# Where the split weights of a narrow matrix product start in memory: 480 bytes or 64 bytes into their tiles

## The chip, the core and the metric

The kernel runs on one core of one Trainium2 chip. The metric is the device time of one execution in microseconds. Every figure of a profile below is from one profiled execution on that core.

## What is computed

A small decoder trunk of two layers on 512 tokens of width 1024, in float32. The part that matters here is the feed forward that ends each layer:

```python
def swiglu(h, w_gate_up, w_down):
    gu = h @ w_gate_up                                   # 1024 -> 2 * 2816
    return (jax.nn.silu(gu[..., :D_FF]) * gu[..., D_FF:]) @ w_down

x = x + swiglu(rms_norm(x, ln_ffn[layer]), w_gate_up[layer], w_down[layer])
```

Ahead of it stand, in layer 0, a gated delta rule mixer, in layer 1 a sliding-window attention, in both an attention to 256 memory tokens and an output projection.

## The kernel before

Activations lie transposed, 128 features on the partitions by 512 tokens, eight tiles for the width of 1024. A product with a weight matrix runs on TensorE in a reduced float32 format, so both operands are split in two: a high part `hi` (a copy into that format, by ScalarE, line 140) and a low part `lo` (the source minus the high part, by VectorE, line 153). One step of a product is then three matmuls (`mm3`, line 146): high weights by high input, high weights by low input, low weights by high input. Each is preceded by a weight load of its own, 128 columns of 4 bytes, that is 512 bytes in each partition.

Most products are **wide**: the moving input has 512 tokens. In the gate and up products of the feed forwards all but the first few columns go by **quarters** (`quarters`): two blocks of 128 columns are taken together, their weights and the inputs are cut into 2 by 2 quarters, and seven products of sums of quarters take the place of eight. The matmuls of these products are **narrow**: 256 tokens, four steps of three matmuls for a product. The inputs of the quarters are the high and low parts `h`, `l` of the normed activations, or sums of their quarters in tiles called `T`. The results go into the accumulators `g`.

The split weights of a quarter product are 512 columns wide. They come from `ring`: six places, cut from three pairs of tiles `whi`, `wlo` of 1152 elements. Each tile is the two halves of 1024 elements and 128 elements more, so that a place of 640 elements has room for 512 at any start up to 128:

```python
places.extend(tuple(x[:, i * T:(i + 1) * T + P] for x in two) for i in range(2))
...
return [x[:, shift[0]:shift[0] + T] for x in places[-1]]
```

`shift[0]` is set in `begin`, which starts one pair of column blocks. In each layer `begin` runs 19 times: nine times in the first half of the feed forward (four for gates, five for ups), ten in the second. The wide products use tiles of the same names from their first element on.

**Addresses.** What follows from the program's allocation, counted in bytes modulo 512 within a partition: all tiles `whi`, `wlo` of the shared pool start at 320, and so do `h`, `l` and `T` in both feed forwards. A quarter's input begins at a whole multiple of 1024 bytes in its tile, a step's weights at a whole multiple of 512 bytes after the place's start. So in all narrow matmuls of the feed forwards the weights lie 480 bytes beyond the input modulo 512, which is 32 bytes before it. In the wide products of the feed forwards the distance is 0. Distances in the rest of the program, between the moving operand and the weights that are loaded beside it, for narrow matmuls of the same format: in the first 40 us the products of the memory tokens have 128 (where `mh`, `ml` at 192 move past weights at 320), 384 (where weights at 320 in `whi`, `wlo` move past `mh`, `ml` as the loaded side) and 96 (the same with a pair `whi`, `wlo` of the early pool at 96). In the last 30 us the down products of the last two output blocks run in two halves of 256 tokens, at distance 0.

The order of the matmuls on TensorE is that of the program. The splits for the next products run ahead on ScalarE and VectorE, through the ring. The raw weights come by DMA from the SP queue (and two accumulating DMAs for each pair from GpSimd's queue).

Of the kernel before, what the change touches and what calls it, by code (L numbers as in the profile page):

```python
# [18 lines left out]
P = 128  # L19
# [67 lines left out]
class Builder:  # L87
# [1011 lines left out]
    def ffn(self, fp, xp, layer, h, apool, rope=False):  # L1099
# [4 lines left out]
        acts, sums, open_pairs, places, waiting, shift, sized = [], [], [], [], [], [0], []  # L1104
# [34 lines left out]
        def begin(f, up, by, tag, bufs, then):  # L1139

            o = [self.t(fp, [P, T], F32, tag, bufs) for _ in range(2)]
            steps = self.quarters(fp, [col(f + i, up) for i in range(2)], sums, by, o, ring)
            shift[0] = P - 8
            next(steps)
            while waiting:
                x = waiting.pop()
                self.nosync(self.fn(x, x, AF.Silu), self.held)
            end()
            next(steps)
            open_pairs.append((steps, then, o))  # L1150
            return o

        def end():
            if open_pairs:
                steps, then, o = open_pairs.pop()
                next(steps, None)
                for x in o:
                    then(x)
# [8 lines left out]
        for f0 in (0, half):  # L1167
# [7 lines left out]
            for f in range(f0 + 1, f0 + half, 2):  # L1175
                if f == 1:
                    g = []
                    for i in range(2):
                        for _ in range(2 - i):
                            sums.append(self.token_sums(fp, layer, len(sums), h))  # L1180
                        g.append(gate(f + i))
                    sums.append(self.token_sums(fp, layer, len(sums), h))
                else:
                    g = begin(f, 0, (self.rstd, self.rstd), "fg", 4, lambda x: self.fn(x, x, AF.Silu))
                begin(f, 1, g, "fu", 3, put)
# [432 lines left out]
```

## Time and profile before

| what | value |
|---|---|
| time, median of 3 runs | 1130.85 us (1130.81 to 1131.25) |
| span of the profiled execution, first to last instruction | 1129.4 us |
| TensorE busy | 1119.9 us, 99% of the span |
| VectorE busy | 827.6 us, 73% |
| ScalarE busy | 634.4 us, 56% |
| GpSimd busy | 73.2 us, 6% |
| granted TensorE clock, mean | 0.998 |

The profiled execution has no other time than its span; the span lies 1.45 us below the median of the runs, and that is what there is around the first and the last instruction. Busy time of matmuls counts their pipelined, modelled ends, so that the duration of one matmul (279 ns for a narrow one) is more than the distance to the next. The pace of matmuls is therefore read from the distance of starts, or from a stretch of the chain that holds nothing but matmuls, divided by their number.

### The profile page before, as it was taken

To read this page: it belongs to the slowest core of one execution; us is meant where nothing else is said; L and a number is where in the kernel's file an instruction comes from. 1 tells how busy PE (TensorE), PEld (TensorE's weight loads), DVE (VectorE), ACT (ScalarE), POOL (GpSimd) and SP (SyncE) were. 2 spreads that over 40 slices of the span, in tenths; PEclk is the share of its full clock that TensorE was granted. 3 is DMA by queue.
4 is the path that set the end of the run, shared out by engine and by line. 5 is a ranking of instruction groups with operands and counts; after the bars stand their busy time and mean duration, and the time that the engine had idled before them with its cause. 6 is when DMAs were issued, how large, how long until landed. Compare 5 with 4: busy or idle time off the path is not lost.

```text
span 1129.4 us, 19330 instructions
## 1 busy us (share of the span) xinstructions
PE 1119.9 (99%) x7339; PEld 986.1 (87%) x7339; DVE 827.6 (73%) x1553; ACT 634.4 (56%) x1285; POOL 73.2 (6%) x91
## 2 busy tenths in 40 slices
PE   9999999999999999999999999999999999999997
PEld 8888778887899988899988887788999988999986
DVE  7676976577888975588955877839999634889643
ACT  8588664456566632366643555856666422666434
POOL 0000000000021001011000000000111000111001
PEclk9999999999999999999999999999999999999999
DMA  8344252234567536377533321116687533776232
GB/s 314 109 153 149 95 131 86 85 113 145 174 167 195 143 111 169 102 191 195 134 89 102 132 75 38 53 43 180 158 201 185 144 103 105 173 190 156 77 103 87
DMA packets 72401, 151.15 MB, mean 134 GB/s; under 512 B 16956, under 2 KB 18516, under 8 KB 72308
## 3 DMA queue, kind: packets, MB, share of 16 engines
q1 hardware_dynamic: 60884, 129.21, 36.3%
q0 software_dynamic: 11136, 20.45, 11.2%
q8 instruction: 57, 0.93, 0.3%
q14 instruction: 36, 0.29, 0.1%
q10 hardware_dynamic: 288, 0.26, 0.1%
HBM read 142.94 MB, written 6.96 MB: 133 GB/s over the span
## 4 chain that ended last, share of the span: by engine, by line
PE 96%; DVE 2%; ACT 1%; DMA 0%; issue 0%; DVEq 0%; SPq 0%; ACTq 0%
PE pj L146 46%; PE g L146 38%; PE sc L146 6%; PE qk L146 3%; PE pt L146 2%; PE pt L150 1%; PE g L150 1%; DVE big L153 1%; DVE qv L156 0%; DVE btmp L153 0%; DMA early<-in_early 0%; DVE wlo L153 0%; ACT sm L134 0%; DVE T L153 0%; DVE gcr L153 0%
## 5 line engine op out<-in xcount | busy, mean ns | idle before, releaser
L140 ACT ACTIVATE whi<-wraw 128x512 fp32r<-128x512 f32 (+3 forms) x318 | 235.3, 748 | 240.6 <-PE pj L146 164.0
L153 DVE TENSOR_TENSOR wlo<-wraw,whi 128x512 fp32r<-128x512 f32 (+3 forms) x318 | 262.8, 837 | 92.7 <-ACT whi L140 85.2
L146 PE MATMUL pj<-h,whi 128*128 128x512 f32 (+1 forms) x652 | 256.4, 395 | 0.0
L146 PE MATMUL pj<-l,whi 128*128 128x512 f32 (+1 forms) x652 | 254.4, 390 | 0.0
L146 PE MATMUL pj<-h,wlo 128*128 128x512 f32 (+1 forms) x652 | 254.0, 390 | 0.0
L146 PE MATMUL g<-T,whi 128*128 128x256 f32 x1216 | 216.8, 279 | 0.0
L146 PEld LDWEIGHTS g<-T,whi 128*128 128x128 f32 x1216 | 185.1, 188 | 1.3 <-DVE fu L156 1.3
L146 PE MATMUL g<-T,wlo 128*128 128x256 f32 x608 | 169.7, 279 | 0.0
L146 PEld LDWEIGHTS pj<-h,whi 128*128 128x128 f32 x652 | 122.4, 188 | 28.0 <-issue 4.1
L146 PEld LDWEIGHTS pj<-h,wlo 128*128 128x128 f32 x652 | 122.5, 188 | 25.4 <-issue 0.9
L146 PE MATMUL g<-l,whi 128*128 128x256 f32 (+1 forms) x500 | 144.5, 289 | 0.0
L146 PE MATMUL g<-h,whi 128*128 128x256 f32 (+1 forms) x500 | 144.4, 289 | 0.0
L146 PE MATMUL g<-h,wlo 128*128 128x256 f32 (+1 forms) x500 | 144.4, 289 | 0.0
L146 PEld LDWEIGHTS pj<-l,whi 128*128 128x128 f32 x652 | 122.6, 188 | 23.6 <-DVE l L1468 0.3
L146 PEld LDWEIGHTS g<-T,wlo 128*128 128x128 f32 x608 | 114.3, 188 | 0.0
L146 PEld LDWEIGHTS g<-h,whi 128*128 128x128 f32 x500 | 94.0, 188 | 1.9
L146 PEld LDWEIGHTS g<-l,whi 128*128 128x128 f32 x500 | 93.9, 188 | 1.9
L146 PEld LDWEIGHTS g<-h,wlo 128*128 128x128 f32 x500 | 93.9, 188 | 1.8
L1286 POOL DMA_DIRECT2D ws<-in_wgu x38 | 33.5, 881 | 733.0 <-DMA ws<-in_wgu 399.1
L140 ACT ACTIVATE whi<-ws 128x512 fp32r<-128x512 f32 x76 | 48.0, 631 | 42.0 <-PE g L146 35.6
L153 DVE TENSOR_TENSOR wlo<-ws,whi 128x512 fp32r<-128x512 f32 x76 | 52.0, 684 | 5.9 <-ACT whi L140 5.9
L1287 POOL DMA_DIRECT2D ws<-in_wgu x38 | 34.2, 900 | 196.4 <-DVE wlo L153 71.4
(421 smaller groups left out, 1683.2 us busy)
## 6 DMA issues: line engine op xcount, KB each, us to landing
wraw<-in_wgu SPq DMA_DIRECT2D x50, 512.0 KB, 4.4
ws<-in_wgu SPq DMA_DIRECT2D x76, 256.0 KB, 3.4
ws<-in_wgu POOLq DMA_DIRECT2D x76, 256.0 KB, 4.5
wraw<-in_win SPq DMA_DIRECT2D x26, 512.0 KB, 3.6
wraw<-in_wdn SPq DMA_DIRECT2D x32, 384.0 KB, 3.1
wraw<-in_wdn SPq DMA_DIRECT2D x32, 320.0 KB, 2.9
wraw<-in_wgu SPq DMA_DIRECT2D x38, 256.0 KB, 4.0
wraw<-in_wout SPq DMA_DIRECT2D x16, 512.0 KB, 3.6
```

What stands on the lines that cost most here:

```text
L140: self.copied = self.nc.scalar.activation(out, in_, AF.Copy, **kw).ins
L146: return self.nc.tensor.matmul(out, lhsT, rhs, start=start, stop=stop, skip_group_check=more).ins
L150: return self.nc.tensor.transpose(out, in_, self.ident[:k, :k]).ins
L153: return eng.tensor_tensor(out=out, in0=a, in1=b, op=op).ins
L1286: nc.gpsimd.dma_start(s1, a22, accum_op=ALU.add)
L1287: nc.gpsimd.dma_start(s3, a21, accum_op=ALU.add)
```

## The change

One number. The split weights of the quarter products start 16 elements (64 bytes) into their place in place of 120 (480 bytes). Both parts, `whi` and `wlo`, move alike, in both layers. Modulo 512 the weights then lie 64 bytes beyond their inputs. Sizes, engines, order and number of the instructions stay, and so do the tiles and their buffers: the two places in a tile hold elements 16 to 528 and 528 to 1040, where they held 120 to 632 and 632 to 1144.

```diff
             o = [self.t(fp, [P, T], F32, tag, bufs) for _ in range(2)]
             steps = self.quarters(fp, [col(f + i, up) for i in range(2)], sums, by, o, ring)
-            shift[0] = P - 8
+            shift[0] = 16
             next(steps)
             while waiting:
```

## The prediction

> **What bounds the kernel now.** I read the page first: how busy each engine is, and the chain of work that ended last.
>
> ```profile
> span 1129.4 us, 19330 instructions
> PE 1119.9 (99%) x7339; PEld 986.1 (87%) x7339; DVE 827.6 (73%) x1553; ACT 634.4 (56%) x1285; POOL 73.2 (6%) x91
> PE 96%; DVE 2%; ACT 1%; DMA 0%; issue 0%; DVEq 0%; SPq 0%; ACTq 0%
> ```
>
> TensorE is busy for 99% of the span, and the chain runs over it for 96%. So time is won or lost by the pace of the matmuls, wherever nothing else holds them. Next the chain in order of time, whose columns are start, length (both us) and what ran, with the number of instructions merged into the piece. These pieces hold the quarter products of both feed forwards, and three others to compare them with:
>
> ```profile
> 274.49 16.32 PE pj L146 x72
> ...
> 318.53 86.80 PE g L146 x744
> ...
> 472.16 102.05 PE g L146 x852
> ...
> 801.60 86.80 PE g L146 x744
> ...
> 955.21 102.05 PE g L146 x852
> ...
> 1060.08 51.66 PE pj L146 x259
> 1113.43 7.30 PE pj L146 x61
> ```
>
> The pieces of 744 matmuls are narrow ones alone, and each is one unbroken piece: nothing but TensorE itself sets its length. 86.80 / 744 = 116.67 ns from start to start, in layer 0 and in layer 1 alike. The piece of 72 is wide: 16.32 / 72 = 226.67 ns, or 113.33 ns for each 256 tokens. The last piece of 61 is narrow too, in the down product, with weights and inputs at distance 0: 7.30 / 61 = 119.7 ns.
>
> So the same shape of matmul runs at two paces in this trace. The groups of instructions in the two kinds of stretch show the weight loads (columns: count, busy us, mean ns of one, idle before). First the quarter products from 318.53 to 405.33, then the last stage from 1104 to 1111.4:
>
> ```profile
> L146 PEld LDWEIGHTS g<-T,whi 128*128 128x128 f32 x280 | 42.7, 188 | 0.0
> ...
> L146 PEld LDWEIGHTS pj<-l,T 128*128 128x128 f32 x8 | 1.5, 192 | 0.0
> L146 PEld LDWEIGHTS pj<-h,whi 128*128 128x128 f32 x7 | 1.3, 192 | 0.0
> ```
>
> A weight load takes 188 ns at distance 480 and 192 at distance 0. The 4 ns are about the 3 ns by which the paces differ. It goes with the view that the load of the next weights and the stream of the present inputs, which run at the same time, disturb each other in a way that hangs on their distance in memory. That is the only thing the change touches.
>
> **The change part by part.** No instruction is added or taken away, none is moved, and no queue gets more or less. Three things could change.
>
> *The splits.* The copies by ScalarE and the subtractions by VectorE write at other addresses. For the quarter products (start 480, first row of each pair) and wide operands whose tiles begin at distance 0 (second row) the groups are:
>
> ```profile
> L153 DVE TENSOR_TENSOR wlo<-ws,whi 128x512 fp32r<-128x512 f32 x76 | 52.0, 684 | 5.9 <-ACT whi L140 5.9
> L153 DVE TENSOR_TENSOR l<-fu,h 128x512 fp32r<-128x512 f32 x32 | 21.9, 686 | 2.1 <-ACT h L140 1.0
> L140 ACT ACTIVATE whi<-ws 128x512 fp32r<-128x512 f32 x76 | 48.0, 631 | 42.0 <-PE g L146 35.6
> L140 ACT ACTIVATE h<-fu 128x512 fp32r<-128x512 f32 x32 | 20.3, 633 | 19.9 <-DVE fu L153 11.8 <-DVE fu L156 8.1
> ```
>
> 684 against 686 ns and 631 against 633: the start makes nothing of it. I cost this at nothing. The cover is real besides: in the stretch from 318.53 to 405.33, and in a stretch of the last stage to compare, the engines were busy as follows (length, then the busy time of TensorE, weight load, VectorE, ScalarE, GpSimd; granted clock; DMA share).
>
> ```profile
> 318.53:405.33 86.80, 86.80 (x745) 86.80 (x745) 76.86 (x139) 54.19 (x105) 12.22 (x14) 1.00 0.66 165
> 1104.02:1111.46 7.44, 7.44 (x65) 7.44 (x63) 2.61 (x5) 6.63 (x16) 0.00 (x0) 1.00 0.02 8
> ```
>
> VectorE has 9.9 us to spare in 86.8, and TensorE waits for nobody. Were that cover gone, each ns on a VectorE split would cost one ns per product of twelve matmuls, 266 products in all: 0.3 us for each ns. A slower TensorE only widens the cover. A faster one, at the 113.33 ns of a wide matmul's half, would make the stretch 84.3 us long, still over VectorE's 76.9.
>
> *The waits.* The two places of a tile were disjoint and stay so, with the same buffers, so no wait is added or removed: 0.
>
> *The pace of the narrow matmuls.* This is the term that counts. `begin` runs 19 times in each layer, seven products each, four steps, three matmuls: 19 x 7 x 12 x 2 = 3192. The page has the 1824 of them that read `T`:
>
> ```profile
> L146 PE MATMUL g<-T,whi 128*128 128x256 f32 x1216 | 216.8, 279 | 0.0
> L146 PE MATMUL g<-T,wlo 128*128 128x256 f32 x608 | 169.7, 279 | 0.0
> ```
>
> Four of seven products read `T` (the sums t1 to t4), and 1824 x 7 / 4 = 3192. So 1 ns of pace is 3.19 us of time, all on the path.
>
> What pace does distance 64 have? No matmul before stands at 64. The nearest are the narrow products of the memory tokens in the first 40 us. Here are the first and the last start of five unbroken runs (timeline of TensorE; start, length, instruction): two at distance 96, one at 128, one at 384.
>
> ```profile
> 13.54 0.28 PE L146 MATMUL pj<-whi,mh 128*128 128x256 f32 x1
> ...
> 14.85 0.29 PE L146 MATMUL sc<-wlo,mh 128*128 128x256 f32 x1
> ...
> 16.41 0.28 PE L146 MATMUL pj<-whi,mh 128*128 128x256 f32 x1
> ...
> 17.71 0.29 PE L146 MATMUL sc<-wlo,mh 128*128 128x256 f32 x1
> 17.84 0.28 PE L146 MATMUL sc<-mh,whi 128*128 128x256 f32 x1
> ...
> 20.60 0.28 PE L146 MATMUL sc<-mh,wlo 128*128 128x256 f32 x1
> ...
> 26.71 0.29 PE L146 MATMUL pj<-whi,ml 128*128 128x256 f32 x1
> ...
> 32.17 0.28 PE L146 MATMUL pj<-wlo,mh 128*128 128x256 f32 x1
> ```
>
> Distance 96: 11 starts in 1.31 us and 11 in 1.30, together 2.61 / 22 = 118.6 ns. Distance 128: 23 in 2.76 us, 120.0 ns. Distance 384: 46 in 5.46 us, 118.7 ns. With the last stage, distance 0: 119.7 ns. Four distances, all between 118.6 and 120.0, and only 480 has 116.67. It looks as if 480, where the weights stand just behind the inputs, is the exception, and what is gained there goes at any other distance. Distance 64 lies between 0 (119.7) and 96 (118.6), nearer to 96, whose row I take: 118.6 - 116.67 = 1.93 ns, x 3192 = 6.2 us.
>
> Bounds from rows. Above: 120.0 ns, the slowest run, 3.33 x 3192 = +10.6 us. Below: half of a wide matmul, 113.33 ns, the lowest pace per token of this format that the trace has, -3.34 x 3192 = -10.7 us.
>
> *The sum.* 0 + 0 + 6.2 us. Against the profiled execution: 1129.4 + 6.2 = 1135.6 us of span. The median of the runs lies 1.45 us above the span, so 1137.0 us, or 0.5% slower.
>
> The Trainium skill speaks against any effect. Its page "SBUF — State Buffer", section "Who interferes with whom", has it that TensorE never waits on anyone, and "TensorE: Matmul & The Clock Gate", section "Step-by-step: what each phase is for", gives it two independent read ports, one for the stream of inputs and one for the weights. By that the change costs 0 and the time stays at 1130.85 us. The trace does not agree as far as it goes: 116.67 and 119.7 ns for one shape on one engine at one granted clock.
>
> The same page on TensorE, section "Back-to-back issue gap", gives N / 2.4 + 2.5 ns, as an estimate 109.2 ns for 256 tokens. Were distance 64 free of all disturbance, that page's pace would give 23.8 us less, 1107 us. No run here shows narrow matmuls of this format at that pace.
>
> **The rivals.**
>
> *Nothing changes.* Either the pace hangs on something else that goes with the stage (the accumulators `g` in place of `pj`, the traffic beside it), or 64 is as good as 480, being neither 0 nor a large distance. For it: the slower rows are from the first and the last stage, where other things differ too, and only four distances were seen. Against it: in the stretch at 480 the DMA share is 0.66 and VectorE is nearly full, and yet its matmuls are the fastest; in the stretch of the last stage, at distance 0, the DMA share is 0.02, VectorE has 2.61 us of 7.44, and they are slower. Both ran at a granted clock of 1.00. Traffic and clock are not what makes narrow matmuls slow. The time would be 1130.85 us, give or take 1.
>
> *64 is better than 480.* The mechanism: the input stream passes 256 elements while 128 of the weights are loaded, so it gains on them and crosses their place modulo 512 once in each matmul. Weights that start well ahead of it may be met at a moment that costs less than at 480. It decides below 116.0 ns of pace (2.2 us, 0.2%). At the bound of 113.33 ns the time is 1130.85 - 10.7 = 1120.2 us; half way, at 115.0, it is 1125.5. For it: the pace does change with distance, in steps of some ns, and 64 itself was not seen. Against it: distance 96, which is also ahead, has 118.6, and a stream that starts 64 bytes behind should meet the weights sooner, not later. If five distances had been drawn blindly, the sixth would be below the best of them once in six; I give it somewhat more, since no row stands between 0 and 96.
>
> *64 is as bad as 0 or 128.* If everything close to 0 behaves like 0, the pace is 119.7 to 120.0 ns: 3.0 to 3.33 x 3192 = +9.7 to +10.6 us, 1140.6 to 1141.5 us. This has the sign of the forecast.
>
> **How the numbers follow.** A measurement of this kernel can tell about 0.2%, 2.3 us, from no change, that is 0.7 ns of pace. Forecast, a pace near the row of 96 (118.0 to 119.2): 0.40, 1135 to 1139 us. As bad as 0 or 128: 0.20, 1139 to 1141.6. Nothing changes: 0.16. Better than 480: 0.24, of which a third lies above 1125. So slower 0.60, same 0.16, faster 0.24. Predicted is the likeliest, 1137.0 us; its own range is 1135 to 1139. The range that leaves no more than 2 in 10 out reaches from 1125 us (part of the faster case) to 1141.6 us.
>
> **What would show it.** In the profile after, the four pieces of the chain with 744 and 852 matmuls carry the whole difference. By the forecast those of 744 take 88.2 us in place of 86.8 (118.6 x 744), those of 852 some 103.6 (828 narrow ones at 1.93 ns more). The wide pieces stay at 226.67 ns and the last stage at 119.7. The splits stay at 684 and 631 ns; if they moved, the first term was wrong. The weight loads of the quarter products show whether they are disturbed: 188 ns as now, or towards 192. If the chain has waits for VectorE or ScalarE inside the quarter products, the cover was judged wrong. The prediction fails if the pieces of 744 come out at 86.8 us or less.

## The result: 0.3% slower, one nanosecond for each narrow matmul

| | before | after |
|---|---|---|
| time, median of 7 runs each | 1130.91 us (1130.62 to 1131.27) | 1134.22 us (1133.70 to 1134.49) |
| ratio after / before, 95% interval | | 1.0029 [1.0019, 1.0040] |
| span of the profiled execution | 1129.4 us | 1132.5 us |

The change costs 3.3 us. The forecast was +6.2 us (1137.0 us): the right sign and place, nearly twice the size.

The page of the changed kernel, and its chain in order of time (start, length, what ran, number merged):

```profile
span 1132.5 us, 19330 instructions
PE 1123.0 (99%) x7339; PEld 989.8 (87%) x7339; DVE 828.9 (73%) x1553; ACT 635.1 (56%) x1285; POOL 73.0 (6%) x91
...
318.41 87.63 PE g L146 x744
...
472.86 102.96 PE g L146 x852
...
803.11 87.63 PE g L146 x744
...
957.51 102.96 PE g L146 x852
...
1116.59 7.30 PE pj L146 x61
```

The four long pieces are still unbroken. Those of 744 grew from 86.80 to 87.63 us, those of 852 from 102.05 to 102.96; together 2 x 0.83 + 2 x 0.91 = 3.5 us, which is the whole difference of the spans (3.1) and 0.4 more, given back in small stretches between. The piece of 61 at distance 0 has its 7.30 us as before. 87.63 / 744 = 117.78 ns for a narrow matmul, where it was 116.67.

The groups of weight loads and of splits in the first long piece of the changed kernel, and in its whole span (count, busy us, mean ns of one):

```profile
L146 PEld LDWEIGHTS g<-T,whi 128*128 128x128 f32 x280 | 43.2, 190 | 0.0
L146 PEld LDWEIGHTS g<-T,wlo 128*128 128x128 f32 x140 | 26.3, 188 | 0.0
L146 PEld LDWEIGHTS g<-l,whi 128*128 128x128 f32 x108 | 20.7, 192 | 0.0
L146 PEld LDWEIGHTS g<-h,wlo 128*128 128x128 f32 x108 | 20.3, 188 | 0.0
L146 PEld LDWEIGHTS g<-h,whi 128*128 128x128 f32 x107 | 20.1, 188 | 0.0
...
L153 DVE TENSOR_TENSOR wlo<-ws,whi 128x512 fp32r<-128x512 f32 x76 | 52.1, 686 | 6.5 <-ACT whi L140 6.4
...
L140 ACT ACTIVATE whi<-ws 128x512 fp32r<-128x512 f32 x76 | 47.9, 631 | 44.3 <-PE g L146 37.7
```

The splits did not move (686 and 631 ns, against 684 and 631). The weight loads did, and in a strange way: of the three in a step, always the same one takes 192 ns, the load that goes with `l` (and with the second of the two matmuls that read `T` with `whi`, so that their mean is 190), and the other two 188. A disturbance from outside would hardly pick every third matmul for 87 us. This looks like a pattern with a period of three.

A second thing in this trace did not fit one pace for one distance. Between the long pieces stand twelve narrow matmuls at the same distance 64, in layer 1 at 891 us (timeline of TensorE):

```profile
891.71 0.39 PE L146 MATMUL g<-T,whi 128*128 128x256 f32 x2
...
892.61 0.28 PE L146 MATMUL g<-T,wlo 128*128 128x256 f32 x1
892.73 0.40 PE L146 MATMUL pj<-h,whi 128*128 128x512 f32 x1
```

Nine starts in 1.02 us: 113.3 ns, 4.4 ns below the long pieces, at the same distance, in the same program. Of the four stretches of this kind (two in each layer) two end at 113.3 ns and two at 117.8. So three explanations stood beside each other: the distance has a pace (the forecast's); the start address has one; or the first matmuls of a stretch lock into one of several patterns that the distance allows.

### The profile page after: what moved, and what is told of

Read it like the earlier page. It is cut to its first block, busy times and chain, and to the rows that moved or that the text cites. A ratio compares the mean times of both kernels' runs of the same rounds, so it can differ in the third digit from the quotient of the medians.

```text
span 1132.5 us, 19330 instructions
## 1 busy us (share of the span) xinstructions
PE 1123.0 (99%) x7339; PEld 989.8 (87%) x7339; DVE 828.9 (73%) x1553; ACT 635.1 (56%) x1285; POOL 73.0 (6%) x91
## 4 chain that ended last, share of the span: by engine, by line
PE 96%; DVE 2%; ACT 1%; DMA 0%; issue 0%; SPq 0%; DVEq 0%; ACTq 0%
PE pj L146 46%; PE g L146 38%; PE sc L146 6%; PE qk L146 3%; PE pt L146 2%; PE pt L150 1%; PE g L150 1%; DVE big L153 1%; DMA early<-in_early 0%; DVE qv L156 0%; DVE btmp L153 0%; DVE wlo L153 0%; ACT sm L134 0%; ACT whi L140 0%; DVE T L153 0%
## 5 line engine op out<-in xcount | busy, mean ns | idle before, releaser
L146 PEld LDWEIGHTS g<-T,whi 128*128 128x128 f32 x1216 | 187.6, 190 | 1.2 <-DVE fu L156 1.2
```

The lines of the kernel that those rows point to most:

```text
L146: return self.nc.tensor.matmul(out, lhsT, rhs, start=start, stop=stop, skip_group_check=more).ins
```

## Experiments

Where one time stands without a range, it is from one execution; the paces are from its profile.

### Is it the distance or the address? Everything moved

```diff
+        self.t(cp, [P, 24], F32, "moved")            # ahead of all constants
-sized.append(self.t(fp, [P, 40], F32, "rest"))
+sized.append(self.t(fp, [P, 144], F32, "rest"))      # and likewise in the attention of layer 1
```

> The kernel before, with weights and inputs of the feed forwards moved together by 96 bytes: distance 480 as before, but the quarter products' weights start at 384 modulo 512, as they do after the change. If the distance between weights and inputs sets the pace, the quarter products keep 116.67 ns (86.8 us in the unbroken pieces of 744 matmuls). If the start address itself does, they take the 117.78 ns of the changed kernel (87.6 us).

The chain of this kernel has 86.80 us for the 744 and 102.05 us for the 852, to the hundredth what they were before (1130.9 us against 1131.27 for the kernel before beside it). So at this address the start of the weights alone does nothing.

```profile
318.21 86.80 PE g L146 x744
...
471.84 102.05 PE g L146 x852
```

### Two other distances: 0 and 96

```diff
-            shift[0] = 16
+            shift[0] = 0         # distance 0; 24 for distance 96
```

> Quarter weights at the very start of their places, distance 0. By the distance theory the pace is that of the narrow matmuls of the last stage, 119.7 to 120.0 ns, so 89.1 to 89.3 us for a piece of 744, and the kernel is some 10 us above the kernel before. If the last stage was slow for another reason, the pieces stay between 86.8 and 87.6 us.

> Distance 96, the row that the forecast took its price from. By the early rows of the kernel before 118.6 ns (88.2 us for a piece of 744); by those of the changed kernel, where the same runs took 117.3 ns, 87.3 us. If a distance has one pace, all four long pieces agree; if it has several that the first matmuls choose between, the pieces may differ from each other.

Chain at distance 0, then at distance 96:

```profile
318.45 89.27 PE g L146 x744
```

```profile
318.93 87.30 PE g L146 x744
```

At distance 0 89.27 / 744 = 120.0 ns, and the kernel took 1141.24 us, 10.0 above the kernel before beside it (1131.27). The last stage was no special case; the pace of distance 0 holds wherever it stands. At 96 it is 87.30 / 744 = 117.34 ns in all four long pieces (1134.05 us), not the 118.6 ns of the row that the forecast took. That row came from two runs of eleven matmuls; the long pieces are 744.

The Trainium skill, page "SBUF — State Buffer", section "Who interferes with whom", says that TensorE never waits on anyone and gives its two read ports as independent. In the long pieces the chain shows no wait for another engine, so the first is not at issue; against the second the measurement decides: with nothing moved but the start of the weights relative to the inputs, a narrow matmul took 116.67, 117.34, 117.78 or 120.0 ns. Where in the chip the two meet, no run shows.

### Does distance 64 have one pace? An extra matmul ahead of each pair

```diff
             self.split(raw, *w)
+            if begun:                       # first product of a pair; n counts the pairs
+                n = begun.pop()
+                n = 8 + 8 * (n % 19) if n < 38 else 0
+                if n:
+                    self.mm(ps[:, :n], w[0][:, :P], sums[0][b][0][:, :n], True, False, True)
```

> The changed kernel (distance 64) with one extra matmul of 8 to 152 columns ahead of each of the 38 pairs of column blocks; its result is overwritten by the matmul after it. If distance 64 has the one pace of 117.78 ns, every pair has it but for the first few matmuls, and the kernel is 38 x 0.1 to 0.15 us = 4 to 6 us slower than after the change. If the pace is a pattern that locks in by how the first matmuls fall, some pairs run at 113.3 ns, as a stretch of twelve does in the changed kernel's trace at 891 us, and others at 117.78.

1132.89 us, faster than the change although it does 38 matmuls more. Two pairs of this run, one with its first row at 360.00 us and the other at 372.01 (timeline of TensorE; with the added lines, lines 146 and 156 have become 147 and 157):

```profile
360.00 0.39 PE L147 MATMUL g<-T,whi 128*128 128x256 f32 x2
...
362.50 0.28 PE L147 MATMUL g<-l,whi 128*128 128x256 f32 x1
...
372.01 0.28 PE L147 MATMUL g<-l,whi 128*128 128x256 f32 x1
...
374.60 0.28 PE L147 MATMUL g<-h,wlo 128*128 128x256 f32 x1
```

22 starts in 2.50 us, 113.6 ns, and 22 in 2.59 us, 117.7 ns. There is nothing between: 16 of the 38 pairs run at 113.33 ns from their eighth matmul or so to their last, 22 at 117.78. The second layer repeats the first size for size: 8, 40, 64, 80, 104, 112, 128 and 144 columns led to the fast pace in both. So the distance alone does not set the pace: at 64 there are two patterns, and how the first matmuls of a stretch fall (its phase) chooses between them.

### The same at distances 480, 0 and 448

> The kernel before (distance 480) with the same 38 extra matmuls. If the lock can be chosen at every distance, some pairs run at 113.3 ns here too and some at 116.67 or more. If distance 480 has one pattern, all pairs stay at 116.67 ns and the extra matmuls cost 38 x 0.1 = 4 us, 1135 us.

> Distance 0 with the same 38 extra matmuls. If every distance has a fast pattern, some pairs come to 113.3 ns. If distance 0 has one pattern, all stay at 120.0 ns, 1145 us.

> Distance 448, 64 bytes before the inputs, with the same 38 extra matmuls. If only the size of the distance counts, it behaves as 64 does: 113.3 and 117.8 ns. If the side counts (weights ahead of or behind the stream), it behaves as 480: 116.7 ns for all. Nothing in the traces so far says which.

Chains, in this order:

```profile
318.06 88.12 PE g L147 x753
```

```profile
318.26 90.22 PE g L147 x753
```

```profile
318.21 88.62 PE g L147 x753
```

At 480 (1136.38 us) the pairs split too: 20 of the 38 stay at 116.67 ns, 18 at 117.78, so the mean of the piece is 88.12 / 753 = 117.0. None is faster than 116.67. At 0 (1144.85 us) all 38 pairs return to 120.0 within some twelve matmuls. At 448 (1138.32 us) all stay at 117.78; only one stretch of twelve between the long pieces had 113.4, so that a fast pattern which none of the 38 starts reached is not ruled out there. The answer lies between what was expected: the sets of patterns differ by distance. 480 has two patterns and was in its better one. 64 has two, and the change was in its worse one. At 0 one was seen.

The traces show the patterns in two ways, of which neither is enough. Read to the nanosecond, the starts at 480 in the kernel before repeat every four matmuls (distances of about 116, 118, 120 and 113 ns), in the slow pattern of 480 every three, at 96 every five; at 64, 448 and 0 they are even to about 1 ns. The loads show the slow pattern of 64, with every third at 192 ns. In a stretch at 448 with the same 117.78 ns (328 to 336 us) all loads take 187 or 188.

### Choosing the pattern: four extra matmuls

```diff
-                n = 8 + 8 * (n % 19) if n < 38 else 0
+                n = {0: 8, 9: 80}.get(n % 19, 0)
```

> Distance 64 with only four extra matmuls, at the start of each long piece: 8 columns ahead of the first pair of a feed forward, 80 columns ahead of the tenth pair, both sizes that led to 113.3 ns in the run with 38. If the pattern holds once it is locked, the pieces run at 113.33 ns to their end: 84.5 us where the change has 87.6 and before had 86.8, and the kernel takes 1130.9 - 3.34 x 3192 / 1000 + 4 x 0.1 = 1120.6 us. If the matmuls fall back to one pace of the distance, the pieces return to 87.6 us and the time to that of the change, 1134.2 us.

1122.23 us, ratio to before 0.9924 [0.9910, 0.9937]. That is close to what was expected for a pattern that holds. The chain of the profiled execution (which took 1124.62 us):

```profile
318.64 84.44 PE g L147 x745
...
469.90 96.80 PE g L147 x830
...
796.80 20.52 PE g L147 x181
817.32 0.04 issue
817.36 66.67 PE g L147 x564
```

84.44 / 745 = 113.3 ns: the fast pattern held for a whole long piece, 2.4 us below before. In layer 1 it was lost: 20.52 / 181 = 113.4 ns, then a stall, then 66.67 / 564 = 118.2. The view of waits names no engine for the stall (0.2 us, "issue"); the timeline beside it shows what came just before, here and at the same product of the kernel before:

```profile
816.80 0.42 DVE L157 SCALAR_TENSOR_TENSOR fg<-g,fs 128x256 f32<-128x256 f32 x1
817.33 0.30 PEld L147 LDWEIGHTS g<-T,whi 128*128 128x128 f32 x2 [0.20 <-issue]
```

```profile
821.58 0.42 DVE L156 SCALAR_TENSOR_TENSOR fg<-g,fs 128x256 f32<-128x256 f32 x1
822.44 0.40 PE L146 MATMUL g<-T,whi 128*128 128x256 f32 x2
```

The stalled product (`t4` of the pair before) adds into the accumulator that this VectorE instruction still reads, and the program has TensorE wait for it. VectorE ends the read 20.4 us after the start of the long piece in both kernels. Before, the product began 0.44 us after that. At 113.33 ns the 180 matmuls ahead of it take 0.6 us less, and the read comes too late. In layer 0 the same read ends some 1.6 us ahead of the product, and there is no stall.

After it the loads of `wlo` take the 192 ns, another third of them than in the changed kernel, and the pace is 117.78 again:

```profile
L147 PEld LDWEIGHTS g<-T,whi 128*128 128x128 f32 x193 | 29.5, 188 | 0.0
L147 PEld LDWEIGHTS g<-T,wlo 128*128 128x128 f32 x97 | 18.6, 192 | 0.0
L147 PEld LDWEIGHTS g<-h,wlo 128*128 128x128 f32 x73 | 14.0, 192 | 0.0
L147 PEld LDWEIGHTS g<-l,whi 128*128 128x128 f32 x74 | 13.9, 188 | 0.0
```

The five times were 1121.51, 1121.80, 1122.23, 1124.46 and 1124.62 us. Losing the pattern at this place costs 564 x 4.4 ns = 2.5 us, about the distance between the two groups. Only the run of 1124.62 us was profiled, so that the other slow one lost it here too is not shown.

### What a size does to a pattern that stands, and a fifth extra matmul

> Distance 64 with an extra matmul ahead of each pair again, its columns in an order that asks what each size does to a pattern that already stands: in the first layer 8, 40, 40, 64, 64, 104, 104, 128, 128, 80, 144, 144, 112, 112, 16, 24, 32, 56, 96; in the second 8, 16, 112, 16, 112, 72, 48, 88, 120, 80, 136, 152, 16, 16, 72, 72, 48, 48, 112. If the pattern is set by the extra matmul alone, the second of two equal sizes leaves the pace as the first made it. If it is set by how the extra matmul shifts the pattern before it, the same size takes a fast pattern to the slow one and a slow one to the fast. A size that leads to 113.3 ns from both would hold the kernel there after any stall.

The kernel took 1132.34 us. The slow pattern has three phases (which of the three loads is the long one: each of them is, in some pair), the fast one shows one, and the sizes fit that. From the fast pattern no size went two ways: 16 columns (four tries), 72 (two) and 40, 64, 128 and 144 (one each) led to the slow one. From the slow one 16 and 48 stayed slow, and 104 went once slow and once fast. Of the sizes tried from both, only 112 columns led to the fast pattern from both, in all of its tries.

```diff
-                n = {0: 8, 9: 80}.get(n % 19, 0)
+                n = {0: 8, 9: 80, 19: 8, 22: 112, 28: 80}.get(n, 0)     # five
+                n = {0: 8, 9: 80, 3: 112, 6: 112, 12: 112, 15: 112}.get(n % 19, 0)     # twelve
```

> Distance 64, the four extra matmuls of the earlier run and one of 112 columns, the size that led to 113.3 ns from both patterns, ahead of the fourth pair of layer 1. That is the first place after the stall of 0.2 us at which the earlier run's profile lost the fast pattern. If the stall is what lost it and 112 columns bring it back, a run that loses it pays some 8 us of stretch at 4.4 ns in 118 = 0.3 us instead of 2.5, and the runs lie together at 1121.3 to 1122 us, without those at 1124.5. If the pattern is lost at other places too, the times stay spread from 1121.5 to 1124.6.

> The same with two matmuls of 112 columns in each of the four long pieces, twelve extra matmuls in all. They cost 8 x 0.12 = 1 us more than the four. If stalls occur anywhere, this gives the narrower spread; if only at the one place, it is 0.5 to 1 us slower than the kernel with five.

Five: 1122.23 us (1121.93 to 1123.55), ratio 0.9923 [0.9909, 0.9937]. Twelve: 1123.17 us (1122.73 to 1125.18), ratio 0.9934 [0.9922, 0.9947]. In the profiled run with five the stall stands at its place in layer 1 again, as it does in the one with twelve:

```profile
796.13 20.52 PE g L147 x181
816.65 0.03 issue
816.68 64.28 PE g L147 x565
```

but this time the fast pattern survived it: 64.28 / 565 = 113.8 ns with the stall's first matmuls in it, and the pairs before and after the 112 columns both run at 113.3. So this run does not show that 112 columns repair a loss; that they would rests on the run with sizes. Four of its five times lie together (1121.93 to 1122.23), one at 1123.55. The spread with twelve is not narrow either: 1124.65 and 1125.18 lie some 2 us above the other three, although 112 columns follow in every long piece. If 112 columns repair a loss, one at this place alone does not explain those two. The medians of four and five extra matmuls are the same, and both are 0.8% below before. Why the pattern sometimes survives the stall, and where else time is lost, stays open.

### Wide matmuls at distance 64

```diff
+        at = 0 if pool else 16
-        hi, lo = (self.part(tag, bufs, pool)[:, :n] for tag in tags)
+        hi, lo = (self.part(tag, bufs, pool)[:, at:at + n] for tag in tags)
```

> The kernel with four extra matmuls, and the weights of the wide products too begin 64 bytes into their tiles (distance 64 in place of 0; the last output block, whose tiles have no room, stays at 0). Wide matmuls at distance 0 take 226.67 ns, 13.3 ns over 512 / 2.4; narrow ones locked at distance 64 take 113.33, 6.7 ns over 256 / 2.4. If the excess is a matter of the load alone, once in each matmul, a locked wide matmul comes to 220 ns, and the wide piece of 285 after the first quarter stretch from 64.6 us towards 62.7. If wide matmuls have patterns of their own, other paces appear, 224 to 235 ns as seen at single places.

The same wide piece in the chain of the kernel before, at distance 0, and then in that of this kernel, at distance 64:

```profile
407.51 64.65 PE pj L146 x285
```

```profile
408.34 66.49 PE pj L147 x285
```

Slower: 64.65 / 285 = 226.8 ns at distance 0, and 66.49 / 285 = 233.3 ns at distance 64, as in the other long wide pieces of this run. 1137.37 us in all. The excess is not one price for each load, and distance 0, the worst for narrow ones, is the better of these two for wide ones as they ran here. Whether the wide ones have other patterns at 64, which an extra matmul could choose, was not tried.

The first long piece of layer 1 in this run speaks to the narrow ones:

```profile
805.89 87.74 PE g L147 x745
```

Its extra matmul has the same 8 columns, but the piece runs at 117.78 ns from its first pair on, without a stall. So a size does not lead to one pattern by itself: it depends on what ran before it.

## Why the prediction was right, and where its size was off

*That TensorE's pace alone decides* was right. All of the difference lies in the four long pieces, the wide ones and the last stage kept theirs, and no wait appeared in the changed kernel's pieces.

*That the splits cost nothing* was right: 2 ns at most. The check on the other side held only in part. The prediction compared sums over a whole stretch, 84.3 us against VectorE's 76.9, and so found cover at 113.33 ns. On that sum the fast pattern was fed. But at one product of layer 1 the cover was 0.44 us, and there VectorE's late read of an accumulator stalled TensorE.

*The count*, 3192 narrow matmuls, was right: 1.11 ns x 3192 = 3.5 us, against 3.3 measured.

*The price per matmul* is the step that failed in size: 1.93 ns was taken, 1.11 came. So 1134.22 us fell below the 1135 to 1139 that the forecast gave its own case, though inside its wider range. The price was read as 118.6 ns from the early runs at distance 96, and two things were wrong with that. Distance 96 has 117.34 ns in a long piece. And the early runs were short: the changed kernel, whose first stage is the same program, gave other starts for the same eleven matmuls,

```profile
13.47 0.28 PE L146 MATMUL pj<-whi,mh 128*128 128x256 f32 x1
...
14.76 0.28 PE L146 MATMUL sc<-wlo,mh 128*128 128x256 f32 x1
```

eleven in 1.29 us, 117.3 ns, where the kernel before had 118.6 (1.31 and 1.30 us for eleven). Rows that are not settled had been read as the price of a distance. The premise behind it, one pace for one distance, was the deeper mistake. So the right sign is partly luck: distance 64 fell into its slower pattern, and in its faster one the same change would have gained. The 4 ns between weight loads, which the prediction set beside the 3 ns of pace, do not go with the pace in general: at distance 96 the loads took 188 ns as at 480, and the matmuls were slower.

*The rival "64 is better than 480"* got the smaller chance, and the outcome agreed, but the reason against it (distance 96) was wrong. It would have come true with another phase: distance 64 has a pattern of 113.33 ns, the very bound from below that the prediction worked out from half a wide matmul, and with it the time is 1122 us, near the 1120.2 given for that case. The mechanism that this rival named, the stream crossing the place of the weights, no run shows. *"Nothing changes"* fell with the result, and its reason, that the stage sets the pace, with distance 0, where the same stage took 120.0 ns. *"As bad as 0"* fell with 117.78.

## What to carry to other kernels

When TensorE is the bound and the pace of equal matmuls differs between stages, compare the starts in long unbroken pieces. Starts whose distances repeat with a short period, or loads of which every third is 4 ns longer, are here the sign of a locked pattern; but some patterns show neither (448). Before a layout of operands is judged by its time, see whether it has more than one such pattern; an extra matmul of some columns at the start of a stretch is a cheap way to ask. Here four of them took the new layout from 0.3% above before to 0.8% below. What they gain is fragile: the same size did not lead to the fast pattern after wide matmuls at distance 64, and in one run a stall of 0.2 us ended it. A faster pace also uses up cover that a sum over a stretch does not show, so look for the product with the least. Judge narrow and wide products apart: distance 0 was the worst for the one and the better of two for the other.

## What the runs showed of the hardware that was not expected

Each price stands in ns from start to start of narrow matmuls (128 by 256, weights loaded for each): 113.33 and 117.78 at distance 64, 116.67 and 117.78 at 480, 117.78 at 448, 117.34 at 96 (where no extra matmul was tried), 120.0 at 0. The patterns hold for more than 700 matmuls and over the borders of products, and a stall of 0.2 us can end one. Why the patterns exist, what the chip does every third load, and why the distances have just these, no run here shows. The Trainium skill's page "TensorE: Matmul & The Clock Gate", section "Back-to-back issue gap", gives N / 2.4 + 2.5 ns for a single warm matmul, by which 256 columns would take 109.2 ns as an estimate; the lowest that any run held is 113.33.
